# Weights split into two halves 128 bytes apart, and another order of the six products of a K tile

## The chip, the core and the metric

The kernel runs on one core of one Trainium2 chip. The metric is the device time of one execution in microseconds (us), the median over runs. In the profile PE is TensorE's matmuls, PEld its weight loads, DVE VectorE, ACT ScalarE, POOL GpSimd and SP the engine that issues most DMAs.

## The reference

One layer of a hybrid decoder: a combined input projection, a gated short convolution (A), a gated delta rule over 8 heads (B), two merge gates, an output projection, and a feed-forward part with squared ReLU. There are 256 prompt tokens and 32 sample tokens, 288 in all; the model width is 2048 and the inner width 8192. All is float32.

```
proj = x @ w_in                                  # 2048 -> 11280 columns, split into the parts below
conv_out, new_conv_a = causal_depthwise_conv(gC * h, conv_a_buf, conv_a_w)
y_a = (gB * conv_out) @ w_a_out
qkv, new_gdn_buf = causal_depthwise_conv(concatenate([q, k, v], -1), gdn_buf, gdn_conv_w)
...
o, S = gated_delta_rule(qh, kh, vh, g, beta, S0)
...
y_b = o @ w_b_out
merged = sigmoid(m_a) * y_a + sigmoid(m_b) * y_b
x = layer_norm(ALPHA * x + merged @ w_o, ln1_g, ln1_b)
hid = square(relu(x @ w_up))
x = layer_norm(ALPHA * x + hid @ w_down, ln2_g, ln2_b)
```

## The kernel before

Every large product keeps the tokens as moving columns. Weights come in blocks of 512 KB: `raw` is 128 partitions by 4 slices of 256 float32 columns (`KB = 4`, `GW = 256`). A float32 product is made of three products in the type float32r: a value is split into a high part (`hi`, the rounded copy, written by ScalarE in `split_hi`, L184) and a low part (`lo = raw - hi`, written by VectorE in `split_lo`, L139 through the helper `tt`). The activations are kept in the same two parts: `xh` and `xl` for x, `ahl` and `ohl` for the mixers' outputs, `mh` and `ml` for the merged rows, `dh` and `dl` around the first layer norm, `hh` and `hl` for the hidden rows.

`blocks` lists all blocks in order: w_in, w_a_out, w_b_out, w_o, then four rounds of w_up and w_down. For each block, `matmuls(i)` runs over its K tiles (128 rows of the weight) and over two output tiles t = 0 and 1 of 128 columns each. For one K tile these are six products of 128 x 128 weights with 288 moving columns: hi with xh and xl for t = 0, the same for t = 1 (both L216), then lo with xh for t = 0 and t = 1 (L218). The sums stand in `acc`, two PSUM banks, one for each t. In the first round of w_up the moving operand has 290 columns, because layer-norm gain and bias ride along (`NX`).

The order on each engine is the order in which the program is written. The loop at the end runs block by block: the split of a block some steps ahead, the evacuation steps that are due, `matmuls(i)`, and the load of a later block on SP's queue. Steps of the gated delta rule (`gates`, `gdn`) are taken one at a time between blocks by a generator.

**Where things lie in SBUF.** Addresses below are within a partition, as the program was allocated, modulo 256 bytes. Four buffers each of `raw`, `hi` and `lo` have 4,096 bytes. `raw` and `hi` start at 64. A spacer tile of 64 bytes (L1640, `wgap`) stands ahead of `lo`, which starts at 128. Slices are 1,024 bytes apart and output tiles 512, so all weights of `hi` start at 64 and all of `lo` at 128. `xh` starts at 128 and `xl` at 0, and likewise the two parts of each other activation lie 128 apart. A K tile of activations is 288 x 4 = 1,152 bytes, which is 128 modulo 256, so both parts swap places from one K tile to the next. With 290 columns it is 1,160 bytes.

`gates` keeps some ten small tiles (`bs`, `be`, `gu`, `ge`, `gw`, `gea`, `gg`, `by_row`, `gq`, `qt`) in the pool `cp`, which lives for the whole kernel.

Of the kernel before, what the change touches and what calls it, by code (L numbers as in the profile page):

```python
# [9 lines left out]
F32 = mybir.dt.float32  # L10
F32R = mybir.dt.float32r
# [5 lines left out]
P = 128  # L17
# [2 lines left out]
NS = 32  # L20
NT = NP_ + NS
NX = NT + 2
KT = D // P
H = 8
DFF = 8192
# [8 lines left out]
GW = 256  # L34
KB = 4
# [66 lines left out]
def hybrid_kernel(ctx: ExitStack, tc: tile.TileContext, A):  # L102
# [6 lines left out]
    cp = pool("cp")  # L109
    wp = pool("wp", 4)  # L110
# [8 lines left out]
    def nm(s):  # L119
        counter[0] += 1  # L120
        return f"{s}{counter[0]}"
# [13 lines left out]
    act, dve, pe, gps, sp = nc.scalar, nc.vector, nc.tensor, nc.gpsimd, nc.sync  # L135


    def tt(out, a, b, op):
        dve.tensor_tensor(out=out, in0=a, in1=b, op=op)  # L139
# [4 lines left out]
    MUL, ADD, SUB, MIN, MAX = ALU.mult, ALU.add, ALU.subtract, ALU.min, ALU.max  # L144
# [3 lines left out]
    blocks = []  # L148
# [7 lines left out]
    raw, his, los = {}, {}, {}  # L156
# [7 lines left out]
    def load(i, steps=(), between=()):  # L164
# [12 lines left out]
                between.pop(0)()  # L177
        raw[i] = t

    def split_hi(i, step=KB):  # L180
        if i < len(blocks):
            his[i] = wp.tile([P, KB, GW], F32R, tag="hi", name=nm("hi"))
            for k in range(0, KB, step):
                act.copy(his[i][:, k:k + step], raw[i][:, k:k + step])  # L184

    def split_lo(i, step=KB):
        if i < len(blocks):
            los[i] = wp.tile([P, KB, GW], F32R, tag="lo", name=nm("lo"))
            r = raw[i] if blocks[i][0].get("by_token") else raw.pop(i)
            for k in range(0, KB, step):  # L190
                tt(los[i][:, k:k + step], r[:, k:k + step], his[i][:, k:k + step], SUB)

    def matmuls(i):
        gi, r0, k0, first, last = blocks[i]
        if gi.get("by_token"):
            return first_tokens(i, k0)
        members = gi.get("pair", (gi,))
        if first:
            for m in members:
                m["ps"] = acp.tile([P, 2, 512], F32, tag="acc", name=nm("acc"))  # L200
        ps = members[0]["ps"]
        h, l = his.pop(i), los.pop(i)
        ah, al = gi["acts"]()
        n = gi["width"]
        kb = gi["kb"]
        h, l = (u.rearrange("p k c -> p (k c)").rearrange("p (k c) -> p k c", k=kb) for u in (h, l))
        for k in range(kb):
            xh_, xl_ = ah[:, k0 + k, 0:n], al[:, k0 + k, 0:n]
            st = first and k == 0
            en = last and k == kb - 1  # L210
            per = gi["cols"] // P // len(members)
            for u, m in enumerate(members):
                ts = [(m["ps"][:, t, 0:n], slice((per * u + t) * P, (per * u + t + 1) * P)) for t in range(per)]
                both = [(o, c, x) for o, c in ts for x in (xh_, xl_)]
                for o, c, x in both[::2] + both[1::2] if i == 0 else both:
                    pe.matmul(o, h[:, k, c], x, start=st and x is xh_, stop=False)  # L216
                for o, c in ts:
                    pe.matmul(o, l[:, k, c], xh_, start=False, stop=en)  # L218
# [45 lines left out]
    gd = {}  # L264
# [247 lines left out]
    def norms(ps):  # L512
# [517 lines left out]
    G_ = {}  # L1030

    def gates(first):

        xs0 = gd["pool"].tile([P, 12 * NT + KT * 32], F32, tag="S0", name="xf0")
        xf = (xs0[:, 0:12 * NT].rearrange("p (k t) -> p k t", k=12), gd["pool"].tile([P, 4, NT], F32, tag="b4", name="xf1"))
# [20 lines left out]
        bs = cp.tile([P, 3, 16], F32, name="bs")  # L1056
# [3 lines left out]
        be = cp.tile([P, 3, 2, 8], F32, name="be")  # L1060
        beta, g = be[:, :, 0, :], be[:, :, 1, :]
        act.activation(beta, bs[:, :, 0:8], AF.Sigmoid)
        u = cp.tile([P, 3, 8], F32, name="gu")
        e = cp.tile([P, 3, 8], F32, name="ge")
        w = cp.tile([P, 3, 8], F32, name="gw")
        ea = cp.tile([P, 8], F32, name="gea")
# [7 lines left out]
        tt(w, w, e, SUB)  # L1074
        stt(w, u, 0.0, w, MAX, ADD)
        stt(g, w, -1.0, bmid(ea, 3), MUL, MUL)
        gg = cp.tile([P, 96], F32, name="gg")
# [23 lines left out]
        pe.matmul(q[:, 128:136], cst("lcums"), g[:, 2, :], start=True, stop=True)  # L1101
        pe.matmul(q[:, 136:144], cst("lrems"), g[:, 2, :], start=True, stop=True)
        pe.matmul(q[:, 144:272], by_row, cst("lcum"), start=True, stop=True)
        gq = cp.tile([16, P], F32, name="gq")
        ge = cp.tile([P, 96], F32, name="gexp")
        qt = cp.tile([P, 6, 2, 8], F32, name="qt")
# [13 lines left out]
        gw = gsw.rearrange("p (b s) r -> p s b r", s=2)  # L1120
# [515 lines left out]
    aux = []  # L1636
    steps = x_steps(0, 1)
    t0, o0 = steps[0]()
    his[0] = wp.tile([P, KB, GW], F32R, tag="hi", name=nm("hi"))
    wp.tile([P, 16], F32, tag="gap", name="wgap", bufs=1)  # L1640
    los[0] = wp.tile([P, KB, GW], F32R, tag="lo", name=nm("lo"))
    t, h0, l0 = raw.pop(0), his[0], los[0]

    def split_first(k):
        for u in (2 * k, 2 * k + 1):
# [171 lines left out]
```

## Time and profile before

| what | value |
|---|---|
| median of three runs | 1632.31 us (lowest 1631.95) |
| profiled execution, its time | 1632.37 us |
| its span, first to last instruction | 1630.6 us |
| granted TensorE clock, mean | 1.0 |
| HBM read, written | 272.83 MB, 7.63 MB |

The span is what the profile's rows add up to; the execution's own time is 1.8 us longer. The chain of work that ended last belongs to TensorE for 92% of the span, 60% on line L216 and 29% on L218. The matmuls' records overlap, since they are pipelined: a record lasts longer than the distance to the next start. For the pace one therefore divides a stretch of time by the number of matmuls in it, and doesn't read the duration of one.

The DMA engines are busy for 50 to 70% in most slices and move 172 GB/s in the mean; the loads of weights have a median of 3.6 to 3.8 us from issue to landing.

### The profile page before, as it was taken

How to read it: one execution, taken by the hardware profiler on the slowest of the kernel's cores; microseconds unless marked ns; L12 is line 12 of the kernel's file. 1: busy time of each engine (PE TensorE's matmuls, PEld its weight loads, DVE VectorE, ACT ScalarE, POOL GpSimd, SP SyncE). 2: the span in 40 equal slices, each digit the busy share in tenths (PEclk: the TensorE clock that was granted, in tenths of full speed). 3: DMA queues.
4: the chain of work that ended last, by engine and by line, in shares of the span. 5: the costliest groups of instructions: out<-in, count | busy, mean ns of one | idle time of the engine just before them, and what ended most of it. 6: DMA issues, size and time to landing. Idle time of an engine off the chain costs nothing.

```text
span 1630.6 us, 30931 instructions
## 1 busy us (share of the span) xinstructions
PE 1623.6 (100%) x12857; PEld 1610.9 (99%) x12857; DVE 987.2 (61%) x1342; ACT 779.7 (48%) x1215; POOL 139.5 (9%) x286
## 2 busy tenths in 40 slices
PE   9999999999999999999999999999999999999998
PEld 8999999999999999999999999999999999999998
DVE  6787788878544444457776666444444444444566
ACT  7774678367533343344354455443334433344454
POOL 1232214244000000000000000000000000000111
PEclk9999999999999999999999999999999999999999
DMA  8567456846655555555565555555555555555653
GB/s 270 180 175 209 142 175 201 226 120 184 195 169 168 168 168 168 169 167 159 182 206 157 172 165 169 168 168 168 167 168 168 169 168 168 168 168 168 183 164 103
DMA packets 278999, 282.49 MB, mean 173 GB/s; under 512 B 15075, under 2 KB 272920, under 8 KB 278596
## 3 DMA queue, kind: packets, MB, share of 16 engines
q1 hardware_dynamic: 274394, 268.42, 54.8%
q0 software_dynamic: 4032, 11.63, 2.3%
q8 instruction: 101, 1.65, 0.4%
q10 hardware_dynamic: 432, 0.46, 0.1%
q14 instruction: 40, 0.33, 0.1%
HBM read 272.83 MB, written 7.63 MB: 172 GB/s over the span
## 4 chain that ended last, share of the span: by engine, by line
PE 92%; DVE 2%; ACT 2%; DMA 1%; issue 1%; POOL 0%; DVEq 0%; ACTq 0%
PE acc L216 60%; PE acc L218 29%; DMA raw<-in_w_in_dram 1%; DVE lo L139 1%; PE acc L752 1%; ACT hi L184 1%; PE g L1543 0%; PE g L1563 0%; PE g L1566 0%; PE g L1343 0%; PE g L1516 0%; PE g L1555 0%; ACT ao L1605 0%; ACT b L1587 0%; PE g L1352 0%
## 5 line engine op out<-in xcount | busy, mean ns | idle before, releaser
L139 DVE TENSOR_TENSOR lo<-raw,hi 128x1024 fp32r<-128x1024 f32 (+1 forms) x503 | 606.9, 1210 | 542.6 <-ACT hi L184 541.3
L184 ACT CAST hi<-raw 128x1024 fp32r<-128x1024 f32 (+1 forms) x499 | 518.5, 1042 | 704.1 <-PE acc L216 616.6
L216 PE MATMUL acc<-xh,hi 128*128 128x288 f32 x1408 | 394.2, 296 | 0.5 <-ACT xh L961 0.5
L216 PE MATMUL acc<-xl,hi 128*128 128x288 f32 x1408 | 391.9, 295 | 0.0
L218 PE MATMUL acc<-xh,lo 128*128 128x288 f32 x1408 | 298.2, 293 | 0.2 <-DVE lo L139 0.2
L216 PE MATMUL acc<-dl,hi 128*128 128x288 f32 (+1 forms) x1024 | 286.1, 295 | 0.0
L216 PE MATMUL acc<-dh,hi 128*128 128x288 f32 (+1 forms) x1024 | 285.5, 294 | 0.0
L216 PE MATMUL acc<-hl,hi 128*128 128x288 f32 x992 | 276.1, 294 | 0.0
L216 PE MATMUL acc<-hh,hi 128*128 128x288 f32 x992 | 275.5, 293 | 0.0
L216 PEld LDWEIGHTS acc<-xh,hi 128*128 128x128 f32 x1408 | 264.2, 188 | 2.9 <-issue 1.4
L216 PEld LDWEIGHTS acc<-xl,hi 128*128 128x128 f32 x1408 | 263.8, 188 | 0.7
L218 PEld LDWEIGHTS acc<-xh,lo 128*128 128x128 f32 x1408 | 226.2, 188 | 0.4 <-DVE lo L139 0.4
L218 PE MATMUL acc<-dh,lo 128*128 128x288 f32 (+1 forms) x1024 | 217.0, 293 | 0.0
L218 PE MATMUL acc<-hh,lo 128*128 128x288 f32 x992 | 209.1, 292 | 0.0
L216 PEld LDWEIGHTS acc<-dh,hi 128*128 128x128 f32 x1024 | 192.6, 188 | 0.0
L216 PEld LDWEIGHTS acc<-dl,hi 128*128 128x128 f32 x1024 | 192.3, 188 | 0.0
L216 PEld LDWEIGHTS acc<-hh,hi 128*128 128x128 f32 x992 | 186.2, 188 | 0.4 <-issue 0.4
L216 PEld LDWEIGHTS acc<-hl,hi 128*128 128x128 f32 x992 | 185.9, 187 | 0.0
L218 PEld LDWEIGHTS acc<-dh,lo 128*128 128x128 f32 x1024 | 164.6, 188 | 0.0
L218 PEld LDWEIGHTS acc<-hh,lo 128*128 128x128 f32 x992 | 159.2, 188 | 0.0
L216 PE MATMUL acc<-ml,hi 128*128 128x288 f32 x256 | 71.3, 294 | 0.0
L216 PE MATMUL acc<-mh,hi 128*128 128x288 f32 x256 | 71.1, 293 | 0.0
(424 smaller groups left out, 1475.0 us busy)
## 6 DMA issues: line engine op xcount, KB each, us to landing
raw<-in_w_in_dram SPq DMA_DIRECT2D x175, 512.0 KB, 3.7
raw<-in_w_up_dram SPq DMA_DIRECT2D x128, 512.0 KB, 3.8
raw<-in_w_down_dram SPq DMA_DIRECT2D x128, 512.0 KB, 3.6
raw<-in_w_o_dram SPq DMA_DIRECT2D x32, 512.0 KB, 3.6
raw<-in_w_a_out_dram SPq DMA_DIRECT2D x16, 512.0 KB, 3.6
raw<-in_w_b_out_dram SPq DMA_DIRECT2D x16, 512.0 KB, 3.6
out_dram<-S POOLq DMA_DIRECT2D x8, 512.0 KB, 4.1
S<-in_state_gdn_dram POOLq DMA_DIRECT2D x4, 512.0 KB, 5.8
```

Of the source, the lines that this page charges most:

```text
L139: dve.tensor_tensor(out=out, in0=a, in1=b, op=op)
L184: act.copy(his[i][:, k:k + step], raw[i][:, k:k + step])
L216: pe.matmul(o, h[:, k, c], x, start=st and x is xh_, stop=False)
L218: pe.matmul(o, l[:, k, c], xh_, start=False, stop=en)
L752: pe.matmul(out, x[:, kk, c], w[:, k, :], start=False, stop=stop)
```

## The change

**Layout.** `hi` and `lo` become tiles of 2 x 544 columns, 4,352 bytes. The 544-column halves are 2,176 bytes apart, 128 modulo 256. The first half holds the weights of output tile 0 of all four slices, from its 5th column on (`AT = 4`, 16 bytes), the second those of output tile 1. As allocated, `raw`, `hi` and `lo` tiles now start at 128, so the weights of tile 0 start at 144 and those of tile 1 at 16, in `hi` and `lo` alike. `xh` still starts at 128 and `xl` at 0. The last block, whose weights are moving data (`by_token`), keeps the plain layout at the start of the tile.

**Order.** The four products of hi in a K tile are now (t = 0, xh), (1, xh), (1, xl), (0, xl). The two of lo follow as before. The first block loses its special order.

**Space.** The larger tiles take 2 KB more per partition. To make room, the small tiles of `gates` become parts of two buffers, `big` and `small`, in the pool of the gated delta rule, under the tags `kr3` and `kr2`, which its sample part uses later.

```diff
+HALF, AT = 544, 4
...
+    def split_tile(tag, by_token=False):
+        t = wp.tile([P, 2 * HALF], F32R, tag=tag, name=nm(tag))
+        if by_token:
+            return t[:, 0:KB * GW].rearrange("p (k c) -> p k c", k=KB)
+        return t.rearrange("p (t s) -> p t s", t=2)[:, :, AT:AT + KB * P].rearrange("p t (k c) -> p k t c", k=KB)
+
+    def like(view, t):
+        return t.rearrange("p k (t c) -> p k t c", t=2) if len(view.shape) == 4 else t
...
-            his[i] = wp.tile([P, KB, GW], F32R, tag="hi", name=nm("hi"))
+            h = his[i] = split_tile("hi", blocks[i][0].get("by_token"))
+            r = like(h, raw[i])
             for k in range(0, KB, step):
-                act.copy(his[i][:, k:k + step], raw[i][:, k:k + step])
+                act.copy(h[:, k:k + step], r[:, k:k + step])
...
-                both = [(o, c, x) for o, c in ts for x in (xh_, xl_)]
-                for o, c, x in both[::2] + both[1::2] if i == 0 else both:
-                    pe.matmul(o, h[:, k, c], x, start=st and x is xh_, stop=False)
-                for o, c in ts:
-                    pe.matmul(o, l[:, k, c], xh_, start=False, stop=en)
+                r = k * per + u
+                for t, x in ((0, x_), (1, x_), (1, y_), (0, y_)):
+                    pe.matmul(m["ps"][:, t, 0:n], h[:, r, t], x, start=st and x is x_, stop=False)
+                for t in range(2):
+                    pe.matmul(m["ps"][:, t, 0:n], l[:, r, t], x_, start=False, stop=en)
...
+        big = gd["pool"].tile([P, 512], F32, tag="kr3", name="big")
+        small = gd["pool"].tile([P, 256], F32, tag="kr2", name="small")
...
-        by_row = cp.tile([P, P], F32, name="by_row")
+        by_row = part(big, 96, P)
...
-    wp.tile([P, 16], F32, tag="gap", name="wgap", bufs=1)
```

On TensorE, in the last round of w_up, where one block ends and the next begins, before (the number behind a name is the buffer's; x2 means twice in a row):

```order
L216 MATMUL acc1535_13931<-dh_8578,hi1525_13863 128x288
L216 MATMUL acc1535_13931<-dl_8577,hi1525_13863 128x288
L218 MATMUL acc1535_13931<-dh_8578,lo1526_13865 128x288 x2
L216 MATMUL acc1535_13931<-dh_8578,hi1528_13893 128x288
L216 MATMUL acc1535_13931<-dl_8577,hi1528_13893 128x288
```

The same place after:

```order
L224 MATMUL acc1535_13922<-dh_8569,hi1525_13854 128x288 x2
L224 MATMUL acc1535_13922<-dl_8568,hi1525_13854 128x288 x2
L226 MATMUL acc1535_13922<-dh_8569,lo1526_13856 128x288 x2
L224 MATMUL acc1535_13922<-dh_8569,hi1528_13884 128x288 x2
L224 MATMUL acc1535_13922<-dl_8568,hi1528_13884 128x288 x2
```

A K tile's five rows became three: the high part of the activations now runs through both output tiles, then the low part, where high and low took turns for each output tile. The number of matmuls is the same.

On VectorE, in the same round, the subtractions that make `lo` between two steps of an evacuation, before:

```order
L139 TENSOR_TENSOR lo1586_14373<-raw1572_14272,hi1585_14371 128x1024
L139 TENSOR_TENSOR lo1589_14403<-raw1575_14302,hi1588_14401 128x1024
L139 TENSOR_TENSOR lo1592_14433<-raw1581_14337,hi1591_14431 128x1024
L139 TENSOR_TENSOR r21594_14436<-r1593_14435 128x576
L139 TENSOR_TENSOR lo1598_14468<-raw1584_14369,hi1597_14466 128x1024
```

The same place after:

```order
L140 TENSOR_TENSOR lo1586_14364<-raw1572_14263,hi1585_14362 128x4x2x128
L140 TENSOR_TENSOR lo1589_14394<-raw1575_14293,hi1588_14392 128x4x2x128
L140 TENSOR_TENSOR lo1592_14424<-raw1581_14328,hi1591_14422 128x4x2x128
L140 TENSOR_TENSOR r21594_14427<-r1593_14426 128x576
L140 TENSOR_TENSOR lo1598_14459<-raw1584_14360,hi1597_14457 128x4x2x128
```

Nothing moved; the subtraction, like the cast on ScalarE, now handles its 1,024 elements as eight runs of 128. The orders on ScalarE, GpSimd and SP are unchanged too.

More of the change, by code (lines that the diff above doesn't have):

```diff
@@ L1032, in gates, with part @@
     def gates(first):
+        big = gd["pool"].tile([P, 512], F32, tag="kr3", name="big")
+        small = gd["pool"].tile([P, 256], F32, tag="kr2", name="small")
+        def part(t, a, *sh):
+            n = 1
+            for d in sh:
+                n *= d
+            names = "abc"[:len(sh)]
+            v = t[:, a:a + n]
+            return v.rearrange(f"p ({' '.join(names)}) -> p {' '.join(names)}", **{c: d for c, d in zip(names, sh)}) if len(sh) > 1 else v
         xs0 = gd["pool"].tile([P, 12 * NT + KT * 32], F32, tag="S0", name="xf0")
@@ L1055, in gates @@
             pe.transpose(gt[:, t * P:t * P + P], ba[:, c:c + P], ident)
-        bs = cp.tile([P, 3, 16], F32, name="bs")
+        bs = part(small, 0, 3, 16)
         dve.tensor_reduce(out=bs, in_=gt[:, 0:3 * P].rearrange("p (t w d c) -> p t d c w", t=3, w=4, d=2)[:, :, 0],
@@ L1059, in gates @@
         yield
-        be = cp.tile([P, 3, 2, 8], F32, name="be")
+        be = part(small, 48, 3, 2, 8)
         beta, g = be[:, :, 0, :], be[:, :, 1, :]
         act.activation(beta, bs[:, :, 0:8], AF.Sigmoid)
[L1063 to L1066, printed above, removed]
+        u = part(small, 96, 3, 8)
+        e = part(small, 120, 3, 8)
+        w = part(small, 144, 3, 8)
+        ea = part(small, 168, 8)
         tt(u, bs[:, :, 8:16], bmid(arow[:, 1, :], 3), ADD)
@@ L1076, in gates @@
         stt(g, w, -1.0, bmid(ea, 3), MUL, MUL)
-        gg = cp.tile([P, 96], F32, name="gg")
+        gg = part(big, 0, 96)
         g2, gm = gg[:, 0:32].rearrange("p (a b c) -> p a b c", a=2, b=8), gg[:, 32:96].rearrange("p (a b) -> p a b", a=8)
@@ L1103, in gates @@
         pe.matmul(q[:, 144:272], by_row, cst("lcum"), start=True, stop=True)
-        gq = cp.tile([16, P], F32, name="gq")
+        gq = part(big, 224, P)[0:16]
         ge = cp.tile([P, 96], F32, name="gexp")
-        qt = cp.tile([P, 6, 2, 8], F32, name="qt")
+        qt = part(big, 352, 6, 2, 8)
         act.activation(qt[:, 0:2], q[:, 0:32].rearrange("p (q b h) -> p q b h", q=2, b=2), AF.Exp)
@@ L1638, in hybrid_kernel @@
     t0, o0 = steps[0]()
-    his[0] = wp.tile([P, KB, GW], F32R, tag="hi", name=nm("hi"))
-    wp.tile([P, 16], F32, tag="gap", name="wgap", bufs=1)
-    los[0] = wp.tile([P, KB, GW], F32R, tag="lo", name=nm("lo"))
-    t, h0, l0 = raw.pop(0), his[0], los[0]
+    his[0], los[0] = split_tile("hi"), split_tile("lo")
+    t, h0, l0 = like(his[0], raw.pop(0)), his[0], los[0]
     def split_first(k):
```

13 lines of the change are left out of this document (5 added, 8 removed).

## The prediction

> **What bounds the kernel now.** I read the first two parts of the page, then the waits of TensorE, then counted its matmuls by stage. Columns of the first rows: engine, busy us, share of the span, instructions; then tenths busy in 40 equal slices.
>
> ```profile
> PE 1623.6 (100%) x12857; PEld 1610.9 (99%) x12857; DVE 987.2 (61%) x1342; ACT 779.7 (48%) x1215; POOL 139.5 (9%) x286
> DVE  6787788878544444457776666444444444444566
> PEclk9999999999999999999999999999999999999999
> ```
>
> TensorE (PE) is busy for the whole span at the full granted clock. VectorE (DVE) has spare time in every slice, the most loaded showing 8 tenths. The waits of TensorE (who waited for whom, us in total, times, longest) say the same; its rows that concern the products are these two:
>
> ```profile
> PE acc L216 <- ACT xh L961: 0.5, 1, 0.5
> PE acc L218 <- DVE lo L139: 0.2, 1, 0.2
> ```
>
> So no wait can be won here. The time is a number of matmuls times the gap from one start to the next. The number, from the two lines that write the products (a window over the whole span, x is the count):
>
> ```profile
> 0.00:1631.00 1631.00, 1360.88 (x7872) 1146.39 (x7872) 1.00 0.58 173
> 0.00:1631.00 1631.00, 832.13 (x3936) 632.15 (x3936) 1.00 0.58 173
> L216 PE MATMUL acc<-dl,hi 128*128 128x290 f32 x256 | 72.3, 297 | 0.0
> L216 PE MATMUL acc<-dh,hi 128*128 128x290 f32 x256 | 72.3, 297 | 0.0
> L218 PE MATMUL acc<-dh,lo 128*128 128x290 f32 x256 | 55.1, 297 | 0.0
> ```
>
> 7,872 + 3,936 = 11,808 matmuls, of which 768 have 290 moving columns (first part of w_up) and 11,040 have 288. Now the gap: instructions of TensorE in a stretch of the 290-column stage and in a long stretch of 288 columns.
>
> ```profile
> 815.00:905.00 90.00, 90.00 (x673) 1.00 0.59 183
> 920.00:1600.00 680.00, 680.00 (x5188) 1.00 0.55 169
> ```
>
> A matmul lasts over two gaps, so some two of each count only reach in from outside: 680/5,186 = 131.1 ns, 90/671 = 134.1 ns. The span is then 11,040 x 131.1 = 1,447.3, plus 768 x 134.1 = 103.0, plus a rest of 80.3 us (start, gated-delta-rule matmuls, end). The profiled run took 1632.4 us, span and 1.8 us around it, and the median of the runs is 1632.3; I sum against 1632.4.
>
> **Do addresses matter to the gap?** The program's allocation gives the places. Before, the hi halves start at 64 modulo 256 bytes and the lo halves at 128; the two activation tiles start 128 apart. From one K tile to the next the activations move by 1,152 bytes, 128 modulo 256, so over two K tiles the distance from the next weights to the running activations goes through 64, 192, 128 and 0. In the 290-column stage the pitch is 1,160 bytes, and the distances run through all multiples of 8. What both stages look like (duration of one in ns, min/median/max):
>
> ```profile
> L216 PE MATMUL acc<-dh,hi x242: 290/294/295, 1015.1 to 1109.8; 128*128 128x288 f32 x121
> L216 PE MATMUL acc<-dl,hi x242: 293/294/296, 1015.3 to 1109.9; 128*128 128x288 f32 x121
> L218 PE MATMUL acc<-dh,lo x240: 290/292/293, 1015.7 to 1109.4; 128*128 128x288 f32 x120
> L216 PE MATMUL acc<-dh,hi x236: 289/297/303, 814.9 to 909.9; 128*128 128x290 f32 x118
> L218 PE MATMUL acc<-dh,lo x235: 291/297/301, 814.8 to 909.5; 128*128 128x290 f32 x118
> ```
>
> Same instruction, same engines beside it, and yet 290 to 296 ns in one stage and 289 to 303 in the other. Two columns explain little of that: 256-column products last 280 ns (row below) against 292 for 288 columns, 0.4 ns a column, 0.8 for two. So distances move a single matmul by up to 14 ns, and the mean of a stage by 3.7 in duration (297 against the mean of 294, 294 and 292, 293.3), 3.0 in gap: I count 0.8 ns of gap for one of duration.
>
> ```profile
> L752 PE MATMUL acc<-lo,hh x32: 277/280/286, 1609.8 to 1622.3; 128*128 128x256 f32 x32
> ```
>
> What runs beside a matmul is the load of the next weights (timeline: start us, us):
>
> ```profile
> 1050.01 0.29 PE L216 MATMUL acc<-dh,hi 128*128 128x288 f32 x1
> 1050.02 0.19 PEld L216 LDWEIGHTS acc<-dl,hi 128*128 128x128 f32 x1
> 1050.14 0.30 PE L216 MATMUL acc<-dl,hi 128*128 128x288 f32 x1
> 1050.15 0.32 PEld L218 LDWEIGHTS acc<-dh,lo 128*128 128x128 f32 x2
> ```
>
> The load for the matmul at 1050.14 is issued with the start of the one at 1050.01. That makes the distance between running activations and next weights the quantity to look at. The trace shows no record of a collision; this is my reading.
>
> **The change part by part.**
>
> *Layout and order.* After it, the half for output tile 0 starts at 144 modulo 256 and that for tile 1 at 16, in hi and lo. With the order (0,x), (1,x), (1,y), (0,y), lo 0, lo 1, five of the six distances in a K tile are equal: 112 in even K tiles, 240 in odd ones, and the sixth is the other value. No instruction is added, and each matmul still has its load: 11,040 gaps change and nothing else of size. The price of a constant distance isn't in the trace. From below: the shortest matmuls are 290 here and 289 in the other stage (288.2 without two columns), 3.3 to 5.1 under the mean of 293.3; I take 4.2, times 0.8 = 3.4 ns of gap, 11,040 x 3.4 = 37 us less. From above: the longest, 303, less 0.8, is 8.9 over the mean: 7.1 ns of gap, 78 us more. I take the lower side, since at present fast and slow distances alternate, the four in use already beat the mix over all distances (131.1 against 134.1 - 0.8 = 133.3), and an equal distance in nearly every gap gives one regular pattern of conflicts in place of twelve. It is a choice, not a reading. Looser still, two matmuls of 128 columns follow at 0.11 us each (0.22 from row to row below), so the loads alone would allow a gap of 110 ns:
>
> ```profile
> 1611.05 0.38 PE L688 MATMUL g<-cf,r 128*128 128x128 f32 x2
> 1611.27 0.38 PE L717 MATMUL acc<-cf,acc 128*128 128x128 f32 x2
> ```
>
> The page "TensorE: Matmul & The Clock Gate" of the Trainium skill, section "Back-to-back issue gap", gives N/2.4 + 2.5 ns for a warm gap. For 288 columns this is 122.5 ns, an estimate from the page; by it a layout without any conflict would end at about 1537 us. The measured 131.1 lies 8.6 above it.
>
> *The 290-column stage.* Its distances still drift with the pitch of 1,160; the mean over all of them stays: 0, or at most the same 3.4 ns x 768 = 2.6 us.
>
> *Splitting casts.* 493 casts and 493 subtractions write eight runs of 128 in place of one of 1,024.
>
> ```profile
> L139 DVE TENSOR_TENSOR lo<-raw,hi 128x1024 fp32r<-128x1024 f32 x493 | 602.6, 1225 | 542.3 <-ACT hi L184 541.3 <-issue 0.2
> L139 DVE TENSOR_TENSOR hl<-r,hh 128x576 fp32r<-128x576 f32 x32 | 24.0, 751 | 0.0
> L139 DVE TENSOR_TENSOR mg<-acc,sg 128x576 f32<-128x576 f32 x8 | 6.0, 751 | 0.0
> L298 ACT ACTIVATE kq<-w 128x256 f32<-128x256 f32 x16 | 6.6, 412 | 2.8 <-DVE w L142 2.7
> L279 ACT COPY w<-acc 128x256 f32<-128x256 f32 x24 | 8.7, 364 | 0.0
> ```
>
> mg reads two runs out of PSUM and hl one run, both 751 ns: a run costs nothing there. On ScalarE, kq in four runs takes 48 ns more than a plain copy of its size, 12 a run, which is the upper bound: eight runs, 96 ns, 47 us of busy time on ACT (780 of 1631) and as much on DVE (987) if it paid too. Both stay below the span, and TensorE waited 0.2 us for a lo. I cost it at nothing. If that cover were gone, the stretch with 8 tenths of DVE, some 200 us, would show waits at L218 first; a tenth more there is still under full.
>
> *Gate tiles moved.* The gates' small tiles now lie in two buffers of the gdn pool. Same instructions, same order on every queue, SP's and POOL's included. The buffers' next user is the sample part, whose first write of kr is at 171.8 us; the gates' last use of by_row as weights is at 73.4:
>
> ```profile
> L1103 PEld LDWEIGHTS g<-ao,by_row x2: 192/192/192, 73.3 to 73.4; 128*128 128x128 f32 x2
> L1448 POOL CAST kr<-hl x32: 286/291/1262, 171.8 to 350.6; 32x128 fp32r<-32x128 f32 x32
> ```
>
> 100 us lie between: no wait. *Start and end:* in the first block the xl products still come after both xh ones, and the 96 products by token read hi and lo as moving data at other starts, 96 x (277 to 286 against 280), under 0.6 us. All nothing.
>
> Sum: 80.3 + 103.0 + 11,040 x 127.7 = 1,409.8, that is 1,593 us of span, 1,595 as timed.
>
> **The rivals.**
>
> *The distances bring nothing.* In the 290-column stage three matmuls in a row have just the new distances, 112, 240 and 112, from 815.7 us on:
>
> ```profile
> L216 PE MATMUL acc<-dh,hi x2: 291/292/294, 815.7 to 816.0; 128*128 128x290 f32 x2
> L216 PE MATMUL acc<-dl,hi x1: 297/297/297, 815.8 to 815.8; 128*128 128x290 f32 x1
> ```
>
> 294, 297 and 291, mean 294, 293.2 without two columns, against 293.3 now: 1632 us. Against it: their neighbours had other distances, and the same distance 112 gave 294 and 291. A second way to the same verdict is that the new pattern is only another draw, worth the mean over all distances, 133.3: 11,040 x 2.2 = 24 us more, 1657.
>
> The skill has a rule that speaks for this rival. "SBUF — State Buffer", section "SBUF: two separate sides", says that inside the engine side only the port pair shared by VectorE and GpSimd causes contention, and a later table gives the weight load a read port of its own. By it the layout can't matter, and the time stays 1632. The trace disagrees in part: the two stages differ by more than two columns.
>
> *The constant distance is a bad one.* A regular pattern repeats a conflict as well as its absence. If 112 and 240 behave as the longest matmuls do, 303 ns, it is 78 us more, 1711; it decides from a gap of 134.1, 3.0 above now. For it: the maxima above. Against: 291 to 297 at these very distances.
>
> **How the numbers follow.** About 2%, 32.6 us or 3.0 ns of gap, is what a measurement of this kernel can tell from no change. The gain at a constant distance gets 0.50, at 1595; its own range is 1540 to 1600, the low end a gap of 122.8, two and a half times the taken gain, since matmuls among changing neighbours need not show the best. Nothing brought, or another draw: 0.37, from 1600 to 1660. A bad distance: 0.13. The range from 1540 to 1660 leaves out some 2 in 10, most of it above.
>
> **What would show it.** Right: counts of 288-column matmuls in a long stretch after the first w_up part give under 128.1 ns, the medians of hi and lo products fall together, and min and max lie closer. Wrong: a gap of 131 with other medians (distance isn't the cause), or longer hi products with equal lo ones (the order matters). A wait at L226 for lo would show the casts. The forecast fails if the next load doesn't collide with the running activations at all, or if some other pair of reads does.

## The result, and the profile after

| | before | after |
|---|---|---|
| median | 1632.31 us (1631.95 to 1633.58) | 1644.2 us (1643.91 to 1644.51) |
| span of the profiled execution | 1630.6 us | 1642.6 us |
| ratio, 95% interval | | 1.0072 (1.0054 to 1.0089) |

One further execution of the kernel before took 2544.21 us, and the medians and the ratio are of the other ones. The changed kernel is slower by 0.7%, and the interval leaves out 1. A gain of 37 us was forecast. The first parts of the page after (engine, busy us, share of the span, instructions; then tenths busy in 40 slices) look as before:

```profile
PE 1635.6 (100%) x12857; PEld 1622.6 (99%) x12857; DVE 987.6 (60%) x1342; ACT 780.4 (48%) x1215; POOL 137.8 (8%) x286
DVE  6787788878544444457776666444444444444466
PEclk9999999999999999999999999999999999999999
```

TensorE still fills the span at the full granted clock, with as many instructions, and only its own busy time grew, by 12.0 us. Its waits after, all of them (who waited for whom, us in total, times, longest), say that nothing new stops it; no product of the loop is among them:

```profile
PE g L907 <- DVE warm L902: 1.0, 1, 1.0
PE g L980 <- DMA xr<-in_x_prompt_dram: 0.4, 1, 0.4
PE g L822 <- ACT g L819: 0.3, 1, 0.3
PE g L818 <- DVE R L140: 0.2, 1, 0.2
```

So the gap must have grown. The same two windows of TensorE as in the prediction, after:

```profile
815.00:905.00 90.00, 90.00 (x673) 1.00 0.60 189
920.00:1600.00 680.00, 680.00 (x5145) 1.00 0.55 167
```

The 290-column stage has the very count of before, 90/671 = 134.1 ns. In the 288-column stretch 43 matmuls fewer fit: 680/5,143 = 132.2 ns against 131.1. 11,040 gaps of 1.1 ns more are 12.1 us, and the span grew by 12.0. That accounts for the difference, as closely as a gap rounded to 0.1 ns can tell (0.05 ns are 0.6 us). By shape (us busy, mean ns of one, idle before), the products of that stage after:

```profile
L224 PE MATMUL acc<-hl,hi 128*128 128x288 f32 x992 | 212.0, 295 | 0.0
L226 PE MATMUL acc<-hh,lo 128*128 128x288 f32 x992 | 211.3, 294 | 0.0
L224 PE MATMUL acc<-hh,hi 128*128 128x288 f32 x992 | 211.1, 294 | 0.0
```

Before, the same three groups had 294, 292 and 293 ns: a nanosecond or two per record is all that the page of the profile has of it. Finer is the distance from one start to the next, averaged over some 500 repeats of each place in the pattern of two K tiles. This table is worked out from the start times of the 288-column products from w_o on; the standard deviation over the repeats is about half a nanosecond, so every place has one fixed value. Below, such a pattern of gaps that comes back unchanged is called a rhythm. In brackets stands the distance (activations that run, less next weights, modulo 256).

```
            gap in ns after product 1 to 6 of a K tile
before, xh at 128   132.5 (64)   132.5 (192)  131.7 (64)   133.3 (128)  128.3 (0)    132.5 (64)
before, xh at 0     131.7 (192)  130.8 (64)   127.5 (192)  132.5 (0)    131.7 (128)  128.3 (192)
after,  xh at 128   131.7 (112)  131.7 (112)  131.7 (112)  131.7 (112)  131.7 (112)  129.2 (240)
after,  xh at 0     132.5 (240)  130.9 (240)  132.5 (240)  135.8 (240)  135.8 (240)  131.7 (112)
```

The constant distance 112 did give one constant gap, 131.7 ns in six places of six. It isn't a short one. And 240 has gaps from 129.2 to 135.8, as 192 had 127.5 to 132.5 before: the distance alone doesn't say what a gap is.

### The profile page after: what moved, and what is told of

The parts are those of the page before. It is cut to its first block, busy times and chain, and to the rows that moved or that the text cites. A ratio compares the mean times of both kernels' runs of the same rounds, so it can differ in the third digit from the quotient of the medians.

```text
span 1642.6 us, 30933 instructions
## 1 busy us (share of the span) xinstructions
PE 1635.6 (100%) x12857; PEld 1622.6 (99%) x12857; DVE 987.6 (60%) x1342; ACT 780.4 (48%) x1215; POOL 137.8 (8%) x286
## 4 chain that ended last, share of the span: by engine, by line
PE 98%; ACT 0%; DVE 0%; POOL 0%; issue 0%; ACTq 0%
PE acc L224 63%; PE acc L226 31%; PE acc L760 1%; PE g L1562 0%; PE g L1582 0%; PE g L1585 0%; PE g L1362 0%; PE g L1262 0%; PE g L1535 0%; PE g L1574 0%; PE g L1371 0%; PE g L1066 0%; PE g L714 0%; PE g L1446 0%; PE g L1423 0%; DVE lo L140 0%
## 5 line engine op out<-in xcount | busy, mean ns | idle before, releaser
L224 PE MATMUL acc<-xh,hi 128*128 128x288 f32 x1408 | 303.2, 296 | 0.1
L224 PE MATMUL acc<-xl,hi 128*128 128x288 f32 x1408 | 301.0, 295 | 0.1
L224 PEld LDWEIGHTS acc<-xh,hi 128*128 128x128 f32 x1408 | 224.3, 188 | 2.9 <-issue 1.3
L224 PEld LDWEIGHTS acc<-xl,hi 128*128 128x128 f32 x1408 | 225.6, 189 | 0.3 <-DVE xl L140 0.3
L224 PE MATMUL acc<-dl,hi 128*128 128x288 f32 (+1 forms) x1024 | 219.0, 295 | 0.0
L224 PE MATMUL acc<-dh,hi 128*128 128x288 f32 (+1 forms) x1024 | 218.9, 295 | 0.0
L224 PE MATMUL acc<-hl,hi 128*128 128x288 f32 x992 | 212.0, 295 | 0.0
L224 PE MATMUL acc<-hh,hi 128*128 128x288 f32 x992 | 211.1, 294 | 0.0
L224 PEld LDWEIGHTS acc<-dh,hi 128*128 128x128 f32 x1024 | 163.5, 188 | 0.0
L224 PEld LDWEIGHTS acc<-hh,hi 128*128 128x128 f32 x992 | 157.7, 188 | 0.4 <-issue 0.4
```

The source lines that it names most:

```text
L224: pe.matmul(m["ps"][:, t, 0:n], h[:, r, t], x, start=st and x is x_, stop=False)
```

## The experiments

Three theories stood at first: A, the distance sets the gap; B, the order of the products does; C, the sequence as a whole, with no rule for a single pair. D came after the first three runs: there is a floor near 131 ns with a small spread above it, in which each layout is another draw.

### The order alone

```diff
-                both = [(o, c, x) for o, c in ts for x in (xh_, xl_)]
-                for o, c, x in both[::2] + both[1::2] if i == 0 else both:
+                for t, x in ((0, xh_), (1, xh_), (1, xl_), (0, xl_)):
+                    o, c = ts[t]
```

> The order of the change alone, in the layout of before. Theory A (the distance between the running activations and the next weights sets the gap): the distances of a K tile are the same set in another order, 64 three times, 192, 128 and 0, so the gap of a 288-column product stays near 131.1 ns and the time near 1632 us. Theory B (the order itself costs, for instance by how the two PSUM banks take turns): the whole loss comes with it, 132.2 ns and about 1644 us. Theory C (neither: the sequence of addresses as a whole, with no simple rule): anything from 130 to 133 ns, 1620 to 1655 us.

Measured: 1643.38 us, ratio 1.0066 (1.0052 to 1.0080). Windows of TensorE in two 288-column stretches; the first row is of the kernel before, the others of this run (for the second stretch before, 5,188, see the prediction):

```profile
430.00:700.00 270.00, 270.00 (x2059) 1.00 0.57 167
430.00:700.00 270.00, 270.00 (x2045) 1.00 0.57 168
920.00:1600.00 680.00, 680.00 (x5145) 1.00 0.55 167
```

5,145 again, 132.2 ns. With hi at 64 and lo at 128 as before, hence no constant distance, the order alone brings the whole loss of gap.

### The layout alone

The changed kernel's tiles, with the order of before.

```diff
-                for t, x in ((0, x_), (1, x_), (1, y_), (0, y_)):
+                for t, x in ((0, x_), (1, x_), (1, y_), (0, y_)) if i == 0 else ((0, x_), (0, y_), (1, x_), (1, y_)):
```

> The layout of the change with the order of before (the first block keeps the new order). Theory A: distances are 112 three times and 240 three times in each K tile, and by the gaps after the change (131.7 ns at 112, 132.7 in the mean at 240) this gives 132.2 ns and 1644 us. Theory B (order): 131.1 ns and 1632 us. Theory C: anything from 130 to 133 ns.

Measured: 1641.14 us, ratio 1.0054 (1.0041 to 1.0067).

```profile
75.00:92.00 17.00, 17.00 (x130) 1.00 0.76 245
272.00:320.00 48.00, 48.00 (x367) 1.00 0.77 211
910.00:1600.00 690.00, 690.00 (x5241) 1.00 0.55 168
```

The layout alone costs nearly as much, 8.7 us against 10.9, and the two don't add up. Neither the 1644 us of theory A nor the 1632 us of theory B came. The rows show more: 690/5,239 is 131.7 and 48/365 is 131.5 ns, but 17/128 is 132.8, at the same distances and in the same order. From start times, the 143 products from 74 to 93 us have a gap of 133.35, the 383 from 95 to 146 us one of 131.69.

### Pairs at one distance

The kernel before, with a trial in the first round of w_up: 24 equal products in a row, whose sums nobody reads, for each place of the weights; then with fewer weight columns and other lengths.

```diff
+    def trial(w, seq, n=24, cols=P, N=NT, out=None):
+        outs = [gtile() for _ in range(out or 1)]
+        for j in range(n):
+            a, f = seq[j % len(seq)]
+            pe.matmul(outs[j % len(outs)][0:cols, 0:N], w[:, a:a + cols], ph["dhf"][:, f:f + N], start=j < len(outs), stop=j >= n - len(outs))
```

> The kernel of before with 55 extra runs of 24 matmuls each in the first round of w_up, whose sums nobody reads: one pair of addresses for weights and activations, repeated. 32 runs go through 16 places of the weights for activations at 128 and at 0 modulo 256; others have loads of 32, 64 and 96 columns in place of 128, other numbers of moving columns, two PSUM banks in turn, or two places in turn. Theory A: the gap depends on the distance alone, equal for both places of the activations, with a good and a bad side some 5 to 10 ns apart; with loads of 32 columns it falls to about 123 ns. Theory B: all 32 runs alike near 131 ns, and two banks in turn differ from one. Theory C: runs differ, but the same distance gives other gaps at the two places of the activations. If the load doesn't matter at all, loads of 32 columns leave the gap at 131.

Mean gaps in ns, from start times; the two values of a distance are for activations at 128 and at 0:

```
distance      gap              distance      gap
112    131.06 / 131.24          64    132.00 / 132.18
176    131.18 / 131.18          48    132.12 / 132.35
208    131.12 / 131.94          80    132.65 / 133.29
  0    131.71 / 131.59         144    133.06 / 133.00
 96    131.71 / 131.59          32    133.29 / 133.24
 16    131.82 / 131.82      160, 128   133.24 to 133.47
240    132.00 / 132.06      224, 192   133.35 to 133.53

weight columns at distance 112, 64, 240:   32: 131.76 130.71 132.06    64: 132.65 131.76 132.18
                                           96: 133.24 132.29 133.29   128: 131.24 131.41 132.00
moving columns N with 128 weight columns:  128: 111.9   192: 111.7   256: 117.8   384: 173.4   512: 229.1
```

Two of these trials in the trace, with 128 weight columns at 112 and with 32 at 64 (count, min/median/max duration in ns, first and last start):

```profile
L750 PE MATMUL g<-dh,hi x22: 292/294/301, 867.6 to 870.4; 128*128 128x288 f32 x22
L750 PE MATMUL g<-dh,hi x21: 292/293/294, 969.3 to 971.9; 128*32 128x288 f32 x21
```

A distance that is repeated has its own gap, much the same from either place of the activations, in a band from 131.1 to 133.5 ns. For equal pairs theory A has the rule right and the size wrong: 2.4 ns where 5 to 10 were expected. No distance comes clearly below the kernel's 131.1, so these trials show nothing that a constant one could win. Nor do two distances in turn give the mean of their gaps: weights at 144 and 16 in turn (distances 240 and 112) take 133.7 ns, at 64 and 128 in turn (64 and 0) 133.4, in both cases more than either distance alone; so does a third of four such trials, and the fourth lies between. Two PSUM banks in turn take 132.2 ns and one bank 132.0, against theory B.

Single values are good to some half a nanosecond: the row of 128 weight columns at distance 64 has 132.00 in one trial and 131.41 in the other. Loads of 32 columns don't bring the gap to 123 ns at the three places tried here; sixteen places follow in the next trial. With 128 or 192 moving columns a row stays at 111.7 to 111.9 ns. I read this as the pace of the loads, which no trial with shorter loads tests. From 256 moving columns on, with 128 weight columns, a moving column costs (229.1 - 173.4)/128 = 0.435 ns, and some 6.4 ns stay over (117.8 - 256 x 0.435).

### What holds the floor

The same kind of trial, loads cut to 32 columns in most, and the moving operand changed.

```diff
+        trial(w, move=x[:, 0:1].to_broadcast([P, NT]))
+        trial(w, move=x[:, 0:2 * NT].rearrange("p (a b) -> p a b", b=2)[:, :, 0])
...
+        trial(one, cols=32, move=bmid(one[:, 0:P], 4), out=slice(0, 512))
+        trial(hmr, cols=32, move=bmid(hmr, 4), out=slice(0, 512))
```

> The kernel of before with 30 extra runs of 24 matmuls in the first round of w_up, whose sums nobody reads, to see what the gap of 131 ns is made of when the load isn't its cause: loads of 32 columns at 16 places; 256, 288, 384 and 512 moving columns with such loads; each matmul starting a new sum in place of adding; another place in the PSUM bank; one moving column read 288 times; moving data in two runs, at every second and at every fourth element; and bfloat16. Theory A: with loads of 32 columns the distance still makes 2 to 3 ns. Theory D: a floor of the stream itself, so that 16 places give 130.5 to 132.5 ns. If the reads of the moving data are the cause, one column read 288 times gives about 123 ns and every fourth element more than 131; if adding into PSUM is the cause, fresh sums give about 123 ns; if it is the type, bfloat16 with 256 columns lies at 109 ns against 117.8 for float32r.

```
gap in ns, from start times
32 weight columns at 16 places, 288 moving        128.9 to 133.3, mean 131.0
plain / each product a new sum / other PSUM place 132.22 / 132.22 / 132.22
moving data in two runs of 144 columns            133.33
one moving column read 288 times                  125.28
every 2nd / every 4th element                     256.67 / 260.0
float32r, 32 weight columns, N = 256, 384, 512    113.9, 175.1, 231.1
bfloat16, N = 256, 512                            109.17, 215.83
```

The first row answers what the load does. The same 16 places with 128 weight columns (the table of pairs, activations at 128) have 131.1 to 133.5 ns, mean 132.4. With a quarter of the columns the mean is 131.0, single places move by -3.5 to +2.2 ns, and the place of the weights still makes 4.4 ns, more than the 2 to 3 of theory A and outside the 130.5 to 132.5 of theory D. One of these places, 32 (distance 96), with 32 and with 128 weight columns (128.9 and 131.7 ns):

```profile
L749 PE MATMUL g<-dh,hi x21: 290/292/294, 869.7 to 872.3; 128*32 128x288 f32 x21
L750 PE MATMUL g<-dh,hi x21: 293/295/296, 870.8 to 873.4; 128*128 128x288 f32 x21
```

So the load has a share in the gap, some 1.4 ns in the mean of 16 places, and not the 8 ns from 131 to 123. With other numbers of moving columns a short load goes either way: 117.8 to 113.9 ns at 256, 173.4 to 175.1 at 384, 229.1 to 231.1 at 512.

Rows of the trace for one column read 288 times, and for 512 moving columns in bfloat16 and in float32r (the dtype column writes it f32):

```profile
L749 PE MATMUL g<-dh,hi x25: 286/287/297, 938.5 to 941.5; 128*128 128x288 f32 x25
L749 PE MATMUL g<-hmr x24: 379/379/379, 960.1 to 965.0; 128*32 128x512 bf16 x24
L749 PE MATMUL g<-hmr x24: 387/392/421, 965.4 to 970.7; 128*32 128x512 f32 x24
```

4.9 us against 5.3 for the same count and length; and bfloat16 runs without any spread (379/379/379). Adding into PSUM and the place there change nothing, and weight loads a little; a spread-out operand doubles the gap, and a repeated column takes 7 ns off it. So I put most of the excess down to reading float32r moving data. It is a reading: in the bfloat16 trials the type of the weights changed too. The page "TensorE: Matmul & The Clock Gate" of the Trainium skill, section "Back-to-back issue gap", gives N/2.4 + 2.5 ns for what it calls the isolated gap at the warm clock: 109.2 for 256 columns and 215.8 for 512. The bfloat16 rows agree to the tenth; float32r lies above, 229.1 to 231.8 for 512.

### 256 layouts

Both orders, sixteen places of hi, four of lo against hi, and output tiles 0 or 128 apart: the twelve products of two K tiles, three times over, for each, all from one hi tile and one dh tile.

```diff
+        for new in (0, 1):
+            for d in (0, 128):
+                for s in (0, 64, 128, 192):
+                    for a in range(0, 256, 16):
...
+                        for rep in range(3):
```

> The kernel of before with 256 extra runs of 36 matmuls in the first round of w_up, whose sums nobody reads: the twelve products of two K tiles, three times over, for each of 256 layouts (16 starts of the hi weights, output tiles 0 or 128 bytes apart, lo shifted by 0, 64, 128 or 192) in the order of before and in the new one. Theory A (distance sets the gap, and a good layout removes most of what lies over 123 ns): the means of the layouts spread over 8 ns or more, and the best stand at 127 ns or below. Theory D (a floor near 131 ns that no layout goes under, and a small spread on top in which each layout is another draw): all means within 130 to 134 ns, the layout of before (131.1 in the kernel) near the low end, that of the change (132.2) in the middle, and no better mean for either order by more than 0.5 ns.

```
mean gap of the last 24 of 36 products, ns
all 256: mean 132.64, standard deviation 0.72, lowest 130.54, highest 134.92
order of before, new order (output tiles 0 apart):    132.60, 132.79
order of before, new order (output tiles 128 apart):  132.69, 132.46

                     trial    kernel (long 288-column stretch)
before               131.08   131.1
the change           132.21   132.2
the order alone      132.21   132.2
the layout alone     132.29   131.7
```

Neither order nor split has a mean of its own beyond 0.3 ns; single layouts differ. Before is among the four lowest of 256. The change is not in the middle, as theory D had it: 47 of the 256 lie below its 132.21, and the median is 132.75. Theory A's spread of 8 ns and its gaps of 127 didn't come. Theory D fits best, though 11 layouts lie above its 134 ns. Three of four kernels are met to a tenth. The trial pointed to better layouts, which the next four kernels tried.

### Four layouts picked from the 256

The best in the order of before, hi at 0 and lo at 128 (spacers; the gates' small tiles as in the change):

```diff
+    cp.tile([P, 32], F32, name="cgap")
...
-    wp.tile([P, 16], F32, tag="gap", name="wgap", bufs=1)
+    wp.tile([P, 32], F32, tag="gap", name="wgap", bufs=1)
```

> The kernel before in its own order, but with hi starting at 0 and lo at 128 modulo 256 (before: 64 and 128), the activations at 128 and 0 as before. Spacers move the tiles, and the gates' small tiles lie in two buffers as in the change, to make room. In the trial of 256 layouts this was the fastest, 130.54 ns (the layout of before: 131.08). Theory D (each layout has a gap of its own, whatever surrounds it, and the trial reads it): 11,040 x 0.54 = 6 us less, about 1626 to 1627 us. Rival E (the trial's half nanoseconds come from the trial's own surroundings and don't carry over): 1632 us or more.

The split layout with both halves on multiples of 128, in the order of before (the order's diff as in "The layout alone"):

```diff
-HALF, AT = 544, 4
+HALF, AT = 544, 0
```

> The split layout of the change with AT = 0 in place of 4 (weights of output tile 0 at 128, of tile 1 at 0, in hi and lo alike), in the order of before. All six distances of a K tile are 0 or 128. The trial gave 130.75 ns. Theory D: 11,040 x 0.33 = 4 us less than before, about 1629 us. Theory A (the distance between running activations and next weights sets the gap, where 128 was among the slowest in the pairs, 133.4, and 0 gave 131.6; the mean 132.5): 15 us more, about 1648 us. Rival E: 1632 to 1644 us.

The changed kernel with the same edit, so in the new order:

> The changed kernel with AT = 0 in place of 4 and nothing else, so in the new order. The trial gave 131.13 ns against 132.21 for the change itself. Theory D: 11,040 x 1.08 = 12 us less than the change, about 1632 us, level with before. Theory A: 1648 us. If the new order itself costs (theory B), it stays near 1643.

The slowest of the 256, hi and lo both at 128, new order (the order's diff as above):

```diff
-    wp.tile([P, 16], F32, tag="gap", name="wgap", bufs=1)
```

> The kernel before in the new order, with hi and lo both starting at 128 modulo 256 and the activations at 128 and 0 (the spacer ahead of lo is gone; the gates' small tiles lie in two buffers as in the change). It was the slowest of the 256 layouts in the trial, 134.92 ns, 3.8 above before. Theory D: 11,040 x 3.83 = 42 us more, about 1675 us. Rival E: a loss like that of the order alone, about 1643 us.

| kernel | time, us | ratio to before | gap by trial | gap, from 920 us |
|---|---|---|---|---|
| hi 0, lo 128 | 1649.4 | 1.0106 (1.0092 to 1.0119) | 130.54 | 132.8 |
| AT = 0, order of before | 1627.08 | 0.9968 (0.9956 to 0.9981) | 130.75 | 130.6 |
| AT = 0, new order | 1636.89 | 1.0028 (1.0018 to 1.0039) | 131.13 | 131.1 |
| the slowest | 1665.03 | 1.0201 (1.0187 to 1.0215) | 134.92 | 134.3 |

Windows of TensorE, of hi 0 and lo 128:

```profile
430.00:700.00 270.00, 270.00 (x2036) 1.00 0.56 166
920.00:1600.00 680.00, 680.00 (x5123) 1.00 0.54 166
```

Of AT = 0 in the order of before (its loop ends earlier, so the window does):

```profile
430.00:700.00 270.00, 270.00 (x2068) 1.00 0.57 168
920.00:1590.00 670.00, 670.00 (x5134) 1.00 0.55 170
```

Of AT = 0 in the new order:

```profile
271.00:319.00 48.00, 48.00 (x368) 1.00 0.77 214
430.00:700.00 270.00, 270.00 (x2036) 1.00 0.56 166
920.00:1600.00 680.00, 680.00 (x5188) 1.00 0.55 168
```

Of the slowest:

```profile
430.00:700.00 270.00, 270.00 (x2014) 1.00 0.56 166
920.00:1600.00 680.00, 680.00 (x5064) 1.00 0.53 165
```

Two forecasts from the trial came out (AT = 0 in the order of before, 5 us under before where 4 were expected; the slowest 33 us over where 42 were), one half (AT = 0 in the new order won 7 of the 12 us), and one failed outright: hi 0, lo 128 lost 17 us where 6 were to be won. The third fence shows how a layout can be half right: 48/366 = 131.1 ns, then 270/2,034 = 132.7, then 680/5,186 = 131.1, in one kernel whose addresses modulo 256 and order are the same throughout. A layout can run in two rhythms.

### Several ways into one layout

The same kind of trial once more, 72 products, twelve times for each of nine layouts, entered each time through one product of another length (64 to 240 moving columns). Three layouts read hi, lo, dh and dl at their real strides.

```diff
+        pe.matmul(outs[1][:, 0:lead], w(0, 0, 0), x(0, 0)[:, 0:lead], start=True, stop=True)
+        for k in range(2 * reps):
...
+            for lead in range(64, 256, 16):
+                trial(w, x, order, lead)
```

> The kernel before with a trial in the first round of w_up, whose sums nobody reads: 72 products of six pairs of K tiles for each of nine layouts, twelve times, each time entered through one product of another length (64 to 240 moving columns). Layouts as in the trial of 256 (all parts read from one hi and one dh tile), and three with hi, lo, dh and dl read at the real strides between slices, output tiles and parts. Steady gap: from the last 24 products. Theory F (an order and its addresses allow several steady rhythms, and the way in decides which one is caught): the layout of the layout-only kernel shows both 131.7 and 133.3, the change with AT = 0 both 131.1 and 132.8, the old order with hi at 0 and lo at 128 both 130.6 and 132.8, whatever the strides; so some layouts have two values among their twelve entries. Theory G (addresses alone set the gap, but with bits above 256): each layout has one value for all twelve entries, and for hi at 0 and lo at 128 it is 130.6 from one tile and 132.8 at real strides. Before (hi at 64, lo at 128): 131.1 at real strides by G; by F there may be a second value, and the change then lost by the rhythm it caught. For the change, 132.2 alone would say that its loss is its own; a second value near 131 that it was the way in.

```
gap of the last 24 of 72 products, ns                       twelve entries
before, from one tile, and at real strides                  131.1 all, both
the change                                                  132.2 all
the order alone, at real strides                            132.2 all
the layout alone                                            133.33 nine, 131.67 three
AT = 0, order of before                                     130.55 nine, 131.67 three
AT = 0, new order                                           132.8 six, 131.1 six
hi 0 and lo 128, from one tile, and at real strides         132.8 all, both
```

Two entries of the layout alone in the timeline of TensorE (start us, us, then line, operands, shape, count); the product ahead has 144 moving columns in the first, 160 in the second:

```profile
1373.32 0.23 PE L748 MATMUL g<-dh,hi 128*128 128x144 f32 x1
1373.39 9.80 PE L752 MATMUL g<-dh,hi 128*128 128x288 f32 x72
1383.04 0.24 PE L748 MATMUL g<-dh,hi 128*128 128x160 f32 x1
1383.12 9.70 PE L752 MATMUL g<-dh,hi 128*128 128x288 f32 x72
```

The same 72 products at the same addresses take 9.80 or 9.70 us, by nothing but the product ahead of them. (The PSUM banks change from entry to entry too, two pairs in turn; both times come with either pair.) Theory F holds in the main, and most kernels are read by it: the layout alone moves between 131.67 and 133.33 (131.7 and 133.35 in its trace), AT = 0 in the new order between 131.1 and 132.8 (as in the fence above), hi 0 and lo 128 has 132.8 alone, where theory F expected 130.6 beside it. The slowest of the 256 was not entered in several ways. Theory G falls: some layouts have two values, and in the two layouts read both ways the real strides change nothing. Before and the change have one rhythm each in all twelve ways. What the change lost is thus its own and no accident of the way in. The gain of AT = 0 in the order of before is in part such an accident: three of its twelve entries end at 131.67, above the 131.1 of before, and the kernel caught 130.6 in its long stretch.

The trial of 256 was too short for hi 0 and lo 128: from six of the twelve entries the gap still moves in the first 36 products (133.25 in the second twelve, 131.92 in the third, then 132.8). It read 130.5 to 130.8 in all of its three passes, though, which no entry here shows. Whether that was a third rhythm or a slow way in stays open.

## Why the prediction was wrong

**What bounds the kernel** was right. The span is the number of matmuls times the gap, before and after, and 11,040 x 1.1 ns gives the loss. The measured 1644 us lie within the stated 1540 to 1660, in the part from 1600 on that stood for the rivals; the forecast gain had the wrong direction.

**The step that failed** is "That makes the distance between running activations and next weights the quantity to look at", and with it the price, "times 0.8 = 3.4 ns of gap, 11,040 x 3.4 = 37 us less". Its ground was that the next load is issued with the start of the running matmul. The runs put three things in its place. The distance doesn't set a gap within a sequence: after the change 240 has gaps from 129.2 to 135.8, two distances in turn cost more than either alone in three of four trials, and the order alone, with the old distances, gave the whole loss. What sets the mean is the rhythm of the whole sequence of addresses, 132.2 ns for the change, and in some layouts also what stands ahead. There were no 3.4 ns to be had: repeated pairs have 131.1 to 133.5, 256 layouts 130.5 to 134.9, and before already ran at 131.1. And the load is a small part of it: with a quarter of its columns the mean gap of 16 places falls from 132.4 to 131.0, and the place still matters. Why a sequence has just the rhythm that it has, and which reads meet in it, stays open.

**How I was misled.** The 3.3 to 5.1 ns of the shortest matmuls under the mean were taken for a state that can be had in every gap. They are the short beats of a rhythm whose other beats are longer: before, 127.5 to 133.3 ns average to 131.1. A minimum of single records was no bound for a mean.

**The rival that came nearest** is "another draw", which shared a chance of 0.37 with "nothing brought". The direction was right; its size, the mean over all distances, 133.3, or 24 us, was twice the 12 us found. The 256 layouts have a mean of 132.6, which by 11,040 x 1.5 ns would have been 17 us. That before "already beat the mix over all distances" stood in the prediction as a reason for a gain. It was a reason against it: a layout among the four best of 256 has less to win than to lose. The rule of "SBUF — State Buffer" in the Trainium skill, section "SBUF: two separate sides", was cited for a layout that can't matter. The trials disagree with that use of it: layouts lie up to 4 ns apart, from 130.5 to 134.9. What in them conflicts, if anything does, no run shows.

**The other steps.** The 290-column stage stayed at 134.1, as said. The casts cost nothing that shows, not even in busy time. The groups of casts and subtractions, before (casts; the subtractions' row stands in the prediction, 602.6 us):

```profile
L184 ACT CAST hi<-raw 128x1024 fp32r<-128x1024 f32 x493 | 516.1, 1049 | 704.1 <-PE acc L216 616.6 <-issue 57.0 <-DMA raw<-in_w_in_dram 15.6
```

and after:

```profile
L195 ACT CAST hi<-raw 128x1024 fp32r<-128x1024 f32 x493 | 515.8, 1048 | 716.1 <-PE acc L224 626.1 <-issue 63.2 <-DMA raw<-in_w_in_dram 14.0
L140 DVE TENSOR_TENSOR lo<-raw,hi 128x1024 fp32r<-128x1024 f32 x493 | 603.1, 1226 | 552.5 <-ACT hi L195 550.5 <-PE acc L226 0.4 <-issue 0.2
```

1,049 and 1,048 ns, 1,225 and 1,226: eight runs of 128 cost what one of 1,024 does, and the upper bound of 96 ns wasn't touched. The moved gate tiles brought no wait to TensorE, and start and end, with all else outside the loop, moved the span by no more than the rounding of the gap lets one see (12.0 against 12.1, with 0.6 either way).

**Of what would show it**, one sign of being right came and was no proof. The durations in the stretch for which the prediction shows those of before:

```profile
L224 PE MATMUL acc<-dh,hi x222: 292/293/296, 1022.0 to 1109.4; 128*128 128x288 f32 x111
L224 PE MATMUL acc<-dl,hi x222: 292/293/298, 1022.2 to 1109.6; 128*128 128x288 f32 x111
L226 PE MATMUL acc<-dh,lo x222: 292/293/299, 1022.5 to 1109.9; 128*128 128x288 f32 x111
```

The medians of hi and lo products did fall together, at 293 where 294, 294 and 292 stood, but minimum and maximum don't lie closer, and the gap grew. So "a gap of 131 with other medians (distance isn't the cause)" is the sign that came nearest, with 132.2 for 131.

## What to carry to other kernels

Where TensorE runs without a wait, read its pace as time over count, and take the shortest record for a beat of a rhythm, not for a pace that can be had. Before building on a collision between two reads, shorten one of them in a trial: here loads of 32 columns would have told that the load is worth some 1.4 ns in the mean, and that the place of the weights matters all the same. A trial of a layout has to run until it is steady, and be entered in several ways, before its half nanoseconds are believed; of the kernels picked here, only AT = 0 in the order of before beats the kernel before, by 0.3%, and it might have caught its slower rhythm.

## What the runs showed of the hardware that was not expected

- A sequence of 288-column float32r products settles into a fixed rhythm with the period of its addresses, repeated within half a nanosecond some 500 times. Some layouts have two, and the product ahead decides which one is caught: 133.33 or 131.67, 132.8 or 131.1, 131.67 or 130.55.
- Of the addresses, the part modulo 256 bytes was enough in the two layouts tried both ways: read from one tile or at real strides, the gaps are equal.
- A row of float32r products with 128 weight columns and 256 to 512 moving columns takes about 0.435 ns a moving column and some 6.4 ns more. One column repeated 288 times took 125.3 ns, every second element 256.7, every fourth 260.0.
- A row of products with 128 weight columns takes 111.7 to 111.9 ns each with 128 moving columns as with 192.
- Loads of 32 weight columns in place of 128 lower the mean gap over 16 places of the weights from 132.4 to 131.0 ns, and the place still makes 4.4 ns.
